# A two-layer hybrid decoder step: decay weights loaded earlier, divisions in a step of their own, other estimates, state work in three insertions

## The chip, the core and the metric

The kernel runs on one core of one Trainium2 chip. Its time is the device time of one launch, in microseconds; before the change the median of three runs is 1157.89 (1155.1 to 1159.74). Five engines with a queue each take part: TensorE (PE in the profile) multiplies, VectorE (DVE), ScalarE (ACT) and GpSimd (POOL) do the elementwise work, and SyncE (SP) issues most transfers. Each engine takes its instructions in the order of its own queue and waits at the first one whose inputs aren't there.

## What is computed

One step of a decoder of two layers, for a prompt of 256 tokens and for 8 samples of 4 tokens with their caches. Both groups go through the same weights as 288 columns of one activation matrix of 1024 rows. Each layer does:

```python
h  = rms(x)
x += W_out( sum_m sigmoid(g_m(h)) * P_m(mixer_m(h)) ),  m in {SWA-GQA+sinks, RG-LRU, GLA}
x += CrossAttn(rms(x), memory K/V)            (4 heads over 256 memory tokens)
x += ConvFFN(rms(x))                          (up-proj -> causal dwconv(3) -> SwiGLU -> down)
```

The change lies in the three mixers. The first is attention in a window of 128 tokens, 8 query heads over 2 key heads, with a sink in the softmax; each sample attends to its cached 128 rows. The second (RG-LRU) is a gated linear recurrence of width 512: two block-diagonal products, sigmoids, an exponential, a square root, and a scan. The third (GLA) is linear attention with a decay, in chunks of 32 tokens:

```python
log_alpha = jax.nn.log_sigmoid((a_c @ p['gla_wa2'] + p['gla_ba']).astype(F32)) / GLA_TAU
q_t = qi * jnp.exp(cum)
k_t = ki * jnp.exp(-cum)
o = jnp.einsum('bhts,bhsv->bhtv', att, vi) + jnp.einsum('bhtd,bhdv->bhtv', q_t, S)
S_new = jnp.exp(last[:, :, 0, :])[..., None] * S + jnp.einsum('bhsd,bhsv->bhdv', ki * jnp.exp(last - cum), vi)
```

For a sample the chunk is its 4 tokens, and `S` is the state that comes in from memory: 8 samples times 4 heads of 64 x 128.

## The kernel before

**The main stream.** The large products run as split fp32: `weights` loads a tile of 512 KB into `wst` (4 buffers), ScalarE rounds it into `whi` (L138), VectorE puts the rest into `wlo` (L139), and `mm3` does three matmuls of 128 x 288 for each block of 128 x 128 (L204 to L206). Such a matmul is called a main matmul below, and places in the program are given by their number: 24 of them use one weight tile. SP issues the tile loads in order, with the smaller loads between them.

**The chains.** Each mixer is a Python generator (`swa`, `lru`, `gla`). A `yield` ends a step, and a step is issued as one piece between two main matmuls. `tick()`, called every few main matmuls, looks at an estimate of the time, `est["pe"]`, and issues the next step of each chain whose `ready` has passed. `account()` keeps the estimate: it adds a duration for each instruction, from its engine and size. So numbers in `account` decide where a step lies among the main matmuls. TensorE's order is fixed by hand in this way; the queues of the other engines are put in order by a scheduler, by priority, and loads may be moved up by `tc.high_priority`.

**What the text below follows.** In layer 0 the chains begin at about main matmul 150, and the mixers end by 1250; layer 1 repeats it at some 3650 more. `gla` begins with L771, which multiplies the low-rank decay input `ac` by `wa2` (its load is L766), then L772 to L777 (log-sigmoid). `swa` takes norms (`head_norm`, whose results go through copies L504 and L505 to the matmul L246), scores (L565), exponentials (L581), divisions by the softmax's sum (L590), transposes (L594) and the product with the values (L604). For the samples: scores L630, softmax L637 to L653, transposes L657 and L658, copies L662 (ScalarE) and L663 (VectorE), products L666 and L670, transposes L677. `lru` has its products at L720 with sigmoids at L721, then L725 and L726 (exponential and tanh), L731 and L734. L1422 is the sigmoid of a branch gate. A change of function on ScalarE can need a table load (ACT_TABLE_LOAD), which the profile lists under the line that follows it. In `gla`, the sample states are loaded, used and updated at L931 to L947, two samples in each of four steps.

The small products write PSUM tiles of a pool of four (`psm`), which come free when the engine that reads them is done.

Of the kernel before, what the change touches and what calls it, by code (L numbers as in the profile page):

```python
# [13 lines left out]
ALU = mybir.AluOpType  # L14
# [7 lines left out]
NB = 8  # L22
# [40 lines left out]
def trunk(ctx: ExitStack, tc: tile.TileContext, a: dict):  # L63
# [32 lines left out]

    def m1(n=T, dt=F32):

        return tp.tile([P, T], dt, tag="m1", bufs=9, name=nm("m1"))[:, :n]

    def g2(w):
        return gp.tile([P, 2, WF], F32, tag="g", name=nm("g")).rearrange("p k t -> p (k t)")[:, :w]
# [43 lines left out]
    def account(i):  # L146

        if not hasattr(i, "engine") or not i.outs or i.opcode == "DMACopy":
            return
        e, n = str(i.engine), 1  # L150
        for _, c in i.outs[0].ap[1:]:
            n *= c
        if i.opcode == "Matmult":
            rows, cols = i.ins[0].ap[0][1], 1
            for _, c in i.ins[1].ap[1:]:
                cols *= c
            if i.ins[0].dtype == F32R:
                c = n / 2400 + 0.012
            elif getattr(i, "is_transpose", False):
                c = 0.109  # L160
            else:
                c = n / 600 * min(1.0, -(-rows // 32) / 4) * min(1.0, -(-cols // 32) / 4)
            est["pe"] = max(est["pe"], est["cur"] or 0.0) + c
            if est["cur"] is not None:
                est["cur"] = est["pe"]
            return
        c = {"EngineType.DVE": 0.1 + n / 850, "EngineType.Activation": 0.22 + n / 1200}.get(e, 0.15 + n / 600)
        cur = est["cur"] if est["cur"] is not None and est["serial"] else est["pe"]
        t = est["busy"][e] = max(est["busy"].get(e, 0.0), cur) + c
        if est["cur"] is not None:  # L170
            est["cur"] = max(est["cur"], t + 0.1)

    nc.push_inst_callback(account)
# [7 lines left out]
    class Chain:  # L181


        def __init__(self, gen):
            self.gen, self.out, self.done, self.ready = gen, None, False, est["pe"]

        def step(self):
            est["cur"] = est["pe"]
# [102 lines left out]
    def head_norm(src, n, scale, nt=T, bw=TB):  # L291

        sq = s5()[:, : n * nt].rearrange("p (j t) -> p j t", t=nt)
        A.activation(sq, src, AF.Square)
        yield
        pss = psm()
        for j in range(n):
            PE.matmul(pss[32 * j : 32 * j + 32, :nt], cc("one32"), sq[:, j], start=True, stop=True, skip_group_check=True)
        yield
        ss = m1(nt)  # L300
        A.copy(ss[: 32 * n], pss[: 32 * n, :nt])
        nb = nt // bw
# [167 lines left out]
    def swa(l, got, Q, KV):  # L470
# [78 lines left out]
        for blk in range(2):  # L549
# [37 lines left out]
            for kv in range(2):  # L587
                for j in range(4):
                    h = kv * 4 + j
                    V.tensor_scalar(pp[kv][:, j, :nk], pp[kv][:, j, :nk], den[:, h : h + 1], None, ALU.mult)  # L590
                for kb in range(blk + 1):
                    ptr = psm()
                    for j in range(4):
                        PE.transpose(ptr[:, j * P : (j + 1) * P], pp[kv][:, j, kb * P : (kb + 1) * P], ident)  # L594
                    if kb == 0:
                        A.copy(ptt[kv][:, kb, :], ptr)
                    else:
                        V.tensor_copy(ptt[kv][:, kb, :], ptr)
                    yield
# [161 lines left out]

    def gla(l, got):

        wa2 = m1(2 * P)
        with tc.high_priority(2 * AHEAD):
            nc.sync.dma_start(wa2, a["wa2"][l])  # L766
        ac = got["ac"]
        zc, za = s5t(), s5t()
        for t in range(2):
            pz = psm()  # L770
            PE.matmul(pz[:, :T], wa2[:, t * P : (t + 1) * P], ac, start=True, stop=True)  # L771
            A.activation(zc[:, t], pz[:, :T], AF.Identity, bias=prm[:, l, C_GBA + t : C_GBA + t + 1])  # L772
        yield

        A.activation(za[:, :2], zc[:, :2], AF.Abs)
# [63 lines left out]
        A.copy(kls, ptr[:, P : 2 * P])  # L839
        yield  # L840

        o = s5()
        os, o = o[:, 8 * P : 9 * P], o[:, : 8 * P].rearrange("p (b i h d) -> p b i h d", b=2, i=2, h=2)
        ss = sm([P, 9], "gss", 1)
# [77 lines left out]
                      skip_group_check=True)  # L922
        V.copy_predicated(atts3, cc("gs").bitcast(I32).rearrange("p (h t) -> p h t", h=4), bc(pa[:, :32], 4))
        yield
        po = psm()
        PE.matmul(po[:, :P], atts, vs, start=True, stop=False, skip_group_check=True)
        for b0 in (0, 4):
            pk = [psm(), psm()]
            for b in (b0, b0 + 2):
                s0 = g2(512).rearrange("p (b h d) -> p b h d", b=2, h=2)  # L930
                nc.sync.dma_start(s0, a["glas"][l, :, b : b + 2])  # L931
                for i in range(2):
                    for h in range(4):
                        PE.matmul(po[32 * h : 32 * h + 32, :P], qg[:, h, 32 * (b + i) : 32 * (b + i) + 32], s0[:, i, h // 2],
                                  start=False, stop=(b + i == NB - 1), skip_group_check=True)
                klm = m1(2 * P).rearrange("p (i d) -> p i d", i=2)
                for i in range(2):
                    V.tensor_scalar(klm[:, i], kls, cc("kb")[:, b + i : b + i + 1], None, ALU.mult)
                for i in range(2):
                    j = b + i - b0  # L940
                    for hp in range(2):
                        rows = slice(hp * 64, hp * 64 + 64)
                        PE.matmul(pk[hp][:, j * P : (j + 1) * P], klm[rows, i], vs[rows], start=True, stop=True)
                for i in range(2):
                    j = b + i - b0
                    for hp in range(2):
                        V.scalar_tensor_tensor(s0[:, i, hp], s0[:, i, hp], elast[:, hp, 8 + b + i : 9 + b + i],  # L947
                                               pk[hp][:, j * P : (j + 1) * P], ALU.mult, ALU.add)
                G.dma_start(a["o_gs"][l, :, b : b + 2], s0)
                yield  # L950
        A.copy(os, po[:, :P])
        A.activation(sqj, po[:, :P], AF.Square, accum_out=ss[:, 8:9])
        yield

        got["gla"] = True

# [374 lines left out]
    def mixers(l):  # L1331
# [37 lines left out]

        pm = psm()  # L1370
        wac = m1(2 * P).rearrange("p (k m) -> p k m", k=KD)
        with tc.high_priority(2 * AHEAD):
            nc.sync.dma_start(wac, a["wac"][l])
        V.tensor_mul(wac, wac, prm[:, l, C_GM : C_GM + KD].unsqueeze(2).to_broadcast([P, KD, 32]))
        for k in range(KD):
            q = 32 * (k % 4)
# [278 lines left out]
```

## Time and profile before

| | |
|---|---|
| median of three runs | 1157.89 us |
| the profiled execution | 1156.28 us |
| its span in the trace | 1154.5 us |
| TensorE busy | 1115.5 us, 97% |
| VectorE, ScalarE, GpSimd busy | 69%, 55%, 22% |
| mean granted TensorE clock | 0.991 of full |

The span is the time from the first to the last instruction in the trace; 1.8 us of the execution lie around it. TensorE runs 97% of the span, so another engine's busy time matters only where TensorE waits for it. A row of a timeline or of the waits gives the time that an engine sat idle ahead of an instruction and what the trace takes for the releaser. A granted clock of 0.50 is TensorE's lower level.

### The profile page before, as it was taken

The page shows a single profiled execution, that of the slowest core. Times are in us where ns is not written, and L with a number is a line of the kernel's source. Part 1 is how long each engine was busy: PE and PEld are TensorE (multiplying, and loading weights), DVE is VectorE, ACT ScalarE, POOL GpSimd, SP SyncE. Part 2 cuts the span into 40 slices and gives each one's busy share as a digit, 9 for nine tenths or more (in the row PEclk, how much of TensorE's full clock was granted, in tenths as well). Part 3 has the DMA queues.
Part 4 walks back from the last instruction along what each step waited for, and adds up shares of the span by engine and source line. Part 5 has one row for each costly group of instructions (what it writes and reads, how often), then busy time and mean ns, then how long its engine had stood idle before and what let it go on. Part 6 is the DMA issues. An engine that isn't in the chain of part 4 may idle for free. (4 is left out here: it accounts for less than half of the span.)

```text
span 1154.5 us, 22367 instructions
## 1 busy us (share of the span) xinstructions
PE 1115.5 (97%) x8846; PEld 1060.2 (92%) x8846; DVE 797.6 (69%) x1454; ACT 630.0 (55%) x971; POOL 258.4 (22%) x426
## 2 busy tenths in 40 slices
PE   9699999999999999999998999999999999999998
PEld 8598789999989999999988987899999899999998
DVE  6666685866665878785466666778576668888743
ACT  6435769444554556564445465674455456656532
POOL 1220100311011355550021201012100014555400
PEclk9899999999999999999999998999999999999999
DMA  8563455567467544556554533645675544555562
GB/s 286 197 192 112 134 165 161 186 193 246 156 217 232 157 147 156 164 150 202 174 167 133 154 97 129 182 166 183 201 246 173 184 141 133 160 164 165 176 197 84
DMA packets 62663, 198.11 MB, mean 172 GB/s; under 512 B 7960, under 2 KB 11768, under 8 KB 62560
## 3 DMA queue, kind: packets, MB, share of 16 engines
q1 hardware_dynamic: 59536, 188.55, 51.5%
q0 software_dynamic: 2880, 8.15, 2.0%
q8 instruction: 69, 1.13, 0.4%
q14 instruction: 34, 0.28, 0.1%
q10 hardware_dynamic: 144, 0.00, 0.0%
HBM read 187.35 MB, written 8.95 MB: 170 GB/s over the span
## 5 line engine op out<-in xcount | busy, mean ns | idle before, releaser
L139 DVE TENSOR_TENSOR wlo<-wst,whi 128x1024 fp32r<-128x1024 f32 (+1 forms) x302 | 370.6, 1229 | 153.1 <-ACT whi L138 152.0
L138 ACT CAST whi<-wst 128x1024 fp32r<-128x1024 f32 (+1 forms) x302 | 312.0, 1035 | 268.2 <-PE mm L205 207.1
L204 PE MATMUL mm<-xh,whi 128*128 128x288 f32 x1488 | 449.2, 302 | 1.5 <-DVE g L1440 1.5
L206 PE MATMUL mm<-xh,wlo 128*128 128x288 f32 x1488 | 443.6, 298 | 0.3 <-DVE wlo L139 0.2
L205 PE MATMUL mm<-xl,whi 128*128 128x288 f32 x1488 | 441.4, 297 | 1.0 <-DVE xl L255 1.0
L204 PEld LDWEIGHTS mm<-xh,whi 128*128 128x128 f32 x1488 | 281.9, 189 | 14.2 <-issue 11.3
L206 PEld LDWEIGHTS mm<-xh,wlo 128*128 128x128 f32 x1488 | 281.5, 189 | 5.0 <-DVE wlo L139 1.3
L205 PEld LDWEIGHTS mm<-xl,whi 128*128 128x128 f32 x1488 | 281.7, 189 | 2.8 <-DVE xl L255 1.9
L204 PE MATMUL mm<-s,whi 128*128 128x288 f32 (+1 forms) x756 | 223.7, 296 | 2.3 <-DVE g L1440 2.3
L205 PE MATMUL mm<-s,whi 128*128 128x288 f32 (+1 forms) x756 | 223.1, 295 | 2.5 <-DVE s L219 2.5
L206 PE MATMUL mm<-s,wlo 128*128 128x288 f32 (+1 forms) x756 | 222.5, 294 | 0.0
L204 PEld LDWEIGHTS mm<-s,whi 128*128 128x128 f32 x756 | 142.3, 188 | 4.5 <-issue 2.3
L205 PEld LDWEIGHTS mm<-s,whi 128*128 128x128 f32 x756 | 142.3, 188 | 4.1 <-DVE s L219 4.0
L206 PEld LDWEIGHTS mm<-s,wlo 128*128 128x128 f32 x756 | 142.2, 188 | 0.5
L1310 DVE SCALAR_TENSOR_TENSOR y<-u,prm,y 128x304 f32<-128x304 f32 x176 | 84.0, 530 | 0.3
L1314 POOL TENSOR_TENSOR m<-y 128x256 f32<-128x256 f32 x44 | 60.6, 1378 | 68.0 <-ACT y L1311 49.8
L218 ACT CAST s<-m 128x288 fp32r<-128x288 f32 (+1 forms) x46 | 19.6, 427 | 78.9 <-POOL m L1315 78.9
L1308 ACT ACTIVATE y<-u,prm 128x304 f32<-128x304 f32 x88 | 51.9, 635 | 11.8 <-DVE u L1301 11.8
L219 DVE TENSOR_TENSOR s<-m,s 128x288 fp32r<-128x288 f32 (+1 forms) x46 | 20.8, 451 | 49.1 <-ACT s L218 49.1
L260 POOL TENSOR_TENSOR s<-s 128x288 f32<-128x288 f32 x20 | 17.6, 879 | 140.0 <-ACT s L259 132.9
L1442 POOL TENSOR_TENSOR g<-g,g 128x576 f32<-128x576 f32 x12 | 25.1, 2092 | 84.4 <-DVE g L1440 60.4
L1294 POOL COPY u<-s 128x32 f32<-128x32 f32 x44 | 41.3, 940 | 0.0
(392 smaller groups left out, 1292.8 us busy)
## 6 DMA issues: line engine op xcount, KB each, us to landing
wst<-in_win SPq DMA_DIRECT2D x98, 512.0 KB, 3.6
wst<-in_up SPq DMA_DIRECT2D x88, 512.0 KB, 3.5
wst<-in_down SPq DMA_DIRECT2D x32, 512.0 KB, 3.6
wst<-in_wbr SPq DMA_DIRECT2D x24, 512.0 KB, 3.5
s<-in_mk SPq DMA_DIRECT2D x16, 512.0 KB, 6.7
wst<-in_wout SPq DMA_DIRECT2D x16, 512.0 KB, 4.1
wst<-in_down SPq DMA_DIRECT2D x16, 384.0 KB, 3.1
g<-in_mv SPq DMA_DIRECT2D x16, 256.0 KB, 3.9
```

What stands on the lines that cost most here:

```text
L138: A.copy(hi[:, :n], st[:, :n])
L139: (E or V).tensor_sub(lo[:, :n], st[:, :n], hi[:, :n].bitcast(F32))
L204: PE.matmul(out, wh, bh, start=first, stop=False)
L205: PE.matmul(out, wh, bl, start=False, stop=False)
L206: PE.matmul(out, wl, bh, start=False, stop=last)
L218: A.copy(hi, src)
L219: V.tensor_sub(lo, src, hi.bitcast(F32))
L1294: G.tensor_copy(us[:, :, :, 0:2], fhist[:, 2 * c : 2 * c + 2])
L1308: A.activation(y[:, i, :WFO], u[:, i, 2:], AF.Identity, scale=w[2], bias=prm[:, l, C_FCB + f : C_FCB + f + 1])
L1310: V.scalar_tensor_tensor(y[:, i, :WFO], u[:, i, j : j + WFO], w[j], y[:, i, :WFO], ALU.mult, ALU.add)
L1314: G.tensor_mul(h[:, :NP_], y[:, 0, :NP_], y[:, 1, :NP_])
L1442: (G if x == 1 or m < KD - 4 else V).tensor_add(acc[m], acc[m], g)
```

## The change

- `wa2` is loaded in `mixers` next to `wac`, with a higher priority. In `gla` both products of L771 come first, then both activations.
- `head_norm` has one more `yield`, behind the copy of the sums.
- In `swa` all divisions of L590 are one step, and the transposes come in the steps after it.
- In `gla` the four loads of the sample states come before the prompt's loop. The products `klm` have a step of their own; then one step has all 32 products with the states, and the first updates; a second has the remaining updates.
- `account` no longer moves TensorE's estimate up to the chain's own time, takes other durations for VectorE and ScalarE, and leaves GpSimd out of a chain's time. A chain's first step waits for VectorE's estimate plus 0.5.
- The pool `m1` has ten buffers in place of nine.

```diff
-            est["pe"] = max(est["pe"], est["cur"] or 0.0) + c
+            est["pe"] += c
             if est["cur"] is not None:
-                est["cur"] = est["pe"]
+                est["cur"] = max(est["cur"], est["pe"])
             return
-        c = {"EngineType.DVE": 0.1 + n / 850, "EngineType.Activation": 0.22 + n / 1200}.get(e, 0.15 + n / 600)
+        c = {"EngineType.DVE": 0.09 + n / 970, "EngineType.Activation": 0.12 + n / 1200}.get(e, 0.15 + n / 600)
...
-        if est["cur"] is not None:
+        if est["cur"] is not None and not (est["serial"] and e == "EngineType.Pool"):
             est["cur"] = max(est["cur"], t + 0.1)
...
-            self.gen, self.out, self.done, self.ready = gen, None, False, est["pe"]
+            self.gen, self.out, self.done = gen, None, False
+            self.ready = max(est["pe"], est["busy"].get("EngineType.DVE", 0.0)) + 0.5
...
                     V.tensor_scalar(pp[kv][:, j, :nk], pp[kv][:, j, :nk], den[:, h : h + 1], None, ALU.mult)
+                yield
+            for kv in range(2):
                 for kb in range(blk + 1):
...
-        wa2 = m1(2 * P)
-        with tc.high_priority(2 * AHEAD):
-            nc.sync.dma_start(wa2, a["wa2"][l])
-        ac = got["ac"]
+        ac, wa2 = got["ac"], got["wa2"]
...
+        s0 = []
+        for b in range(0, NB, 2):
+            s0.append(g2(512).rearrange("p (b h d) -> p b h d", b=2, h=2))
+            nc.sync.dma_start(s0[-1], a["glas"][l, :, b : b + 2])
...
+        klm = []
+        for b in range(0, NB, 2):
+            klm.append(m1(2 * P).rearrange("p (i d) -> p i d", i=2))
+            for i in range(2):
+                V.tensor_scalar(klm[-1][:, i], kls, cc("kb")[:, b + i : b + i + 1], None, ALU.mult)
+        yield
         po = psm()
         PE.matmul(po[:, :P], atts, vs, start=True, stop=False, skip_group_check=True)
+        for b in range(NB):
+            for h in range(4):
+                PE.matmul(po[32 * h : 32 * h + 32, :P], qg[:, h, 32 * b : 32 * b + 32], s0[b // 2][:, b % 2, h // 2],
+                          start=False, stop=(b == NB - 1), skip_group_check=True)
...
         for b0 in (0, 4):
             pk = [psm(), psm()]
-            for b in (b0, b0 + 2):
-                s0 = g2(512).rearrange("p (b h d) -> p b h d", b=2, h=2)
-                nc.sync.dma_start(s0, a["glas"][l, :, b : b + 2])
...
         wac = m1(2 * P).rearrange("p (k m) -> p k m", k=KD)
-        with tc.high_priority(2 * AHEAD):
+        got["wa2"] = m1(2 * P)
+        with tc.high_priority(3 * AHEAD):
             nc.sync.dma_start(wac, a["wac"][l])
+            nc.sync.dma_start(got["wa2"], a["wa2"][l])
```

Three places show what this does to the queues. SP's queue in layer 0, before, from the load of the convolution history on (`wax` is for the recurrence, `swav` and `mk` are caches for the sample attention and the cross attention, `wst` is a weight tile):

```order
L1393 DMA lhist_774<-in_lconv 128x96
L697 DMA s_1717<-in_wax 128x1024
L137 DMA wst_706<-in_win 128x1024
L699 DMA lh_1719<-in_lh 128x32
L617 DMA s_1813<-in_swav 128x1024
L1103 DMA s_3008<-in_mk 128x1024
L766 DMA m_457<-in_wa 128x256
L1103 DMA s_3010<-in_mk 128x1024
```

The same queue after the change, at the load of `wac`:

```order
L137 DMA wst_449<-in_win 128x1024
L1379 DMA m_402<-in_wac 128x256
L1380 DMA m_403<-in_wa 128x256
L137 DMA wst_531<-in_win 128x1024
L137 DMA wst_595<-in_win 128x1024
L467 DMA prm<-in_prm 128x250
```

The load of `wa2` stands thirteen places earlier, ahead of all the others of the first piece.

VectorE's queue in layer 1, at the second block of `swa`, before (`g` with `elast` are updates of the sample states, `s` divided by `den` the softmax, `wlo` the low part of a weight tile):

```order
L947 SCALAR_TENSOR_TENSOR g_8065<-g_8065,elast_7237,sm_8063 128x128
L947 SCALAR_TENSOR_TENSOR g_8065<-g_8065,elast_7237,sm_8064 128x128
L1421 TENSOR_TENSOR g_8129<-mm_7995,rbc_6901 128x2x288
L139 TENSOR_TENSOR wlo_8304<-wst_8302,whi_8303 128x1024
L590 TENSOR_SCALAR s_7782<-s_7782,den_7780 128x256 x2
L590 TENSOR_SCALAR s_7783<-s_7783,den_7780 128x256 x4
```

The same place after (the divisions are L592 there):

```order
L139 TENSOR_TENSOR wlo_8181<-wst_8179,whi_8180 128x1024
L586 TENSOR_TENSOR den_7792<-den_7792,es_7793 128x8
L587 RECIPROCAL den_7792<-den_7792 128x8
L592 TENSOR_SCALAR s_7794<-s_7794,den_7792 128x256 x4
L592 TENSOR_SCALAR s_7795<-s_7795,den_7792 128x256 x4
L954 SCALAR_TENSOR_TENSOR g_7560<-g_7560,elast_7269,sm_8081 128x128
```

The divisions no longer stand behind a gate's product and a weight tile; the state updates come behind them.

ScalarE's queue in layer 1, at the sample attention, before, up to L721 of the recurrence (`es`, `mx`, `den` are the softmax of the samples):

```order
L642 ACT_TABLE_LOAD
L642 ACTIVATE es_8421<-mx_8419,prm 128x2
L644 ACTIVATE m_8418,den_8420<-m_8418,mx_8419 128x132 x2
L138 CAST whi_8617<-wst_8616 128x1024
L1422 ACT_TABLE_LOAD
L1422 ACTIVATE g_8480<-g_8480 128x2x288
L218 CAST s_8333<-s_8332 128x1152
L138 CAST whi_8663<-wst_8662 128x1024
L662 COPY m_8558<-sm_8539 128x256
L721 ACTIVATE s_8544<-sm_8546,prm 128x312
```

After, from the second of the two exponentials of that softmax (L648 there) to the copy that was L662 (L666 there; L725, L729 and L730 are what was L721, L725 and L726):

```order
L648 ACTIVATE m_8530,den_8532<-m_8530,mx_8531 128x132
L725 ACT_TABLE_LOAD
L725 ACTIVATE s_8486<-sm_8564,prm 128x312
L725 ACTIVATE s_8487<-sm_8567,prm 128x312
L729 ACT_TABLE_LOAD
L729 ACTIVATE s_8588<-s_8486,sp_85 128x312 x2
L730 ACTIVATE s_8486<-s_8486,sp_85 128x312 x2
L729 ACTIVATE s_8588<-s_8486,sp_85 128x312
L1429 ACT_TABLE_LOAD
L1429 ACTIVATE g_8598<-g_8598 128x2x288
L730 ACTIVATE s_8486<-s_8486,sp_85 128x312
L666 COPY m_8620<-sm_8583 128x256
```

The copy stood two table loads behind the exponentials' first, ahead of the recurrence; now much of the recurrence, with three table loads, stands between. On TensorE, L630 and L657 have 18 main matmuls between them, where they had 66.

## Rows read from the trace of the kernel before

**Rows 1.** The page's first part: busy us, share of the span, instructions.

```profile
PE 1115.5 (97%) x8846; PEld 1060.2 (92%) x8846; DVE 797.6 (69%) x1454; ACT 630.0 (55%) x971; POOL 258.4 (22%) x426
```

**Rows 2.** TensorE's waits: line and releaser, us in all, times, longest.

```profile
PE sm L771 <- DVE m L509: 9.5, 1, 9.5
PE sm L594 <- DVE s L590: 6.4, 4, 2.3
PE sm L771 <- DVE s L509: 4.1, 1, 4.1
...
PE sm L666 <- DVE m L663: 0.8, 2, 0.4
...
PE sm L926 <- DVE m L923: 0.8, 2, 0.4
...
PE sm L969 <- DVE s L958: 0.7, 2, 0.4
```

**Rows 3.** Timeline of SP's queue, 30 to 35 us: start, duration, instruction.

```profile
33.24 0.33 SPq L766 DMA_DIRECT2D m<-in_wa  x1
```

**Rows 4.** The line L766, first in layer 0, then in layer 1.

```profile
DMA to landing us min/median/max: 7.1/7.1/7.1
...
DMA to landing us min/median/max: 3.5/3.5/3.5
```

**Rows 5.** Timeline of TensorE at L771 in layer 0; idle time before, releaser.

```profile
40.48 1.78 PE L771 MATMUL sm<-m,m 128*128 128x288 f32 x3 [9.54 <-DVE m L509]
```

**Rows 6.** Windows: us, TensorE busy (instructions), granted clock, DMA share, GB/s.

```profile
40.48:44.10 3.62, 3.62 (x11) 0.50 0.58 201
137.00:144.00 7.00, 6.98 (x89) 1.00 0.37 114
609.97:614.10 4.13, 4.13 (x16) 0.59 0.01 2
706.30:713.10 6.80, 6.77 (x42) 0.50 0.40 118
```

**Rows 7.** Timeline of VectorE ahead of L594 in layer 0.

```profile
135.48 1.23 DVE L139 TENSOR_TENSOR wlo<-wst,whi 128x1024 fp32r<-128x1024 f32 x1
```

**Rows 8.** Timeline of ScalarE around L771 in layer 0.

```profile
33.71 0.21 ACT L336 ACTIVATE sl<-prm 128x8 f32<-128x8 f32 x1 [2.21 <-DMA prm<-in_prm]
...
44.03 0.69 ACT L776 ACTIVATE s<-s 128x576 f32<-128x576 f32 x1
```

**Rows 9.** Timeline of ScalarE at the sample attention in layer 1.

```profile
736.24 1.28 ACT L642 ACT_TABLE_LOAD   x1
737.54 0.30 ACT L642 ACTIVATE es<-mx,prm 128x2 f32<-128x2 f32 x1
...
742.50 1.04 ACT L138 CAST whi<-wst 128x1024 fp32r<-128x1024 f32 x1
743.45 0.36 ACT L662 COPY m<-sm 128x256 f32<-128x256 f32 x1
743.81 1.05 ACT L721 ACTIVATE s<-sm,prm 128x312 f32<-128x312 f32 x2
```

**Rows 10.** Timeline of VectorE at the sample attention in layer 1.

```profile
740.90 0.15 DVE L646 TENSOR_TENSOR den<-den,es 128x2 f32<-128x2 f32 x1
...
741.69 0.31 DVE L653 TENSOR_TENSOR pn<-m,cst 128x32 f32<-128x32 f32 x2
```

**Rows 11.** Timeline of TensorE in layer 1: main matmuls, L630, L720.

```profile
702.98 0.29 PE L205 MATMUL mm<-xl,whi 128*128 128x288 f32 x1
...
703.51 0.30 PE L206 MATMUL mm<-xh,wlo 128*128 128x288 f32 x1
...
732.79 0.66 PE L630 MATMUL sm<-s,m 128*32 128x132 f32 x16
...
743.08 1.22 PE L720 MATMUL sm<-s,s 128*128 128x312 f32 x4
```

**Rows 12.** Timeline of ScalarE in layer 0, the recurrence's first L721 and last L726.

```profile
171.63 1.05 ACT L721 ACTIVATE s<-sm,prm 128x312 f32<-128x312 f32 x2
...
186.03 0.99 ACT L726 ACTIVATE s<-s,sp 128x312 f32<-128x312 f32 x2
```

More of the change, by code (lines that the diff above doesn't have):

```diff
@@ L97, in m1 @@
     def m1(n=T, dt=F32):
-        return tp.tile([P, T], dt, tag="m1", bufs=9, name=nm("m1"))[:, :n]
+        return tp.tile([P, T], dt, tag="m1", bufs=10, name=nm("m1"))[:, :n]
     def g2(w):
@@ L762, in gla @@
     def gla(l, got):
-        wa2 = m1(2 * P)
-        with tc.high_priority(2 * AHEAD):
-            nc.sync.dma_start(wa2, a["wa2"][l])
-        ac = got["ac"]
+        ac, wa2 = got["ac"], got["wa2"]
         zc, za = s5t(), s5t()
+        pz = [psm(), psm()]
         for t in range(2):
-            pz = psm()
-            PE.matmul(pz[:, :T], wa2[:, t * P : (t + 1) * P], ac, start=True, stop=True)
-            A.activation(zc[:, t], pz[:, :T], AF.Identity, bias=prm[:, l, C_GBA + t : C_GBA + t + 1])
+            PE.matmul(pz[t][:, :T], wa2[:, t * P : (t + 1) * P], ac, start=True, stop=True)
+        for t in range(2):
+            A.activation(zc[:, t], pz[t][:, :T], AF.Identity, bias=prm[:, l, C_GBA + t : C_GBA + t + 1])
         yield
@@ L924, in gla @@
         yield
+        klm = []
[3 more added lines that the diff above has]
+                V.tensor_scalar(klm[-1][:, i], kls, cc("kb")[:, b + i : b + i + 1], None, ALU.mult)
+        yield
         po = psm()
         PE.matmul(po[:, :P], atts, vs, start=True, stop=False, skip_group_check=True)
+        for b in range(NB):
+            for h in range(4):
+                PE.matmul(po[32 * h : 32 * h + 32, :P], qg[:, h, 32 * b : 32 * b + 32], s0[b // 2][:, b % 2, h // 2],
+                          start=False, stop=(b == NB - 1), skip_group_check=True)
@@ L927, in gla @@
+        A.copy(os, po[:, :P])
+        A.activation(sqj, po[:, :P], AF.Square, accum_out=ss[:, 8:9])
         for b0 in (0, 4):
             pk = [psm(), psm()]
-            for b in (b0, b0 + 2):
-                s0 = g2(512).rearrange("p (b h d) -> p b h d", b=2, h=2)
-                nc.sync.dma_start(s0, a["glas"][l, :, b : b + 2])
[L932 to L950, printed above, removed]
@@ L951, in gla @@
-        A.copy(os, po[:, :P])
-        A.activation(sqj, po[:, :P], AF.Square, accum_out=ss[:, 8:9])
-        yield
+            for j in range(4):
+                for hp in range(2):
+                    rows = slice(hp * 64, hp * 64 + 64)
+                    PE.matmul(pk[hp][:, j * P : (j + 1) * P], klm[(b0 + j) // 2][rows, j % 2], vs[rows], start=True, stop=True)
+            for j in range(4):
+                b = b0 + j
+                for hp in range(2):
+                    V.scalar_tensor_tensor(s0[b // 2][:, b % 2, hp], s0[b // 2][:, b % 2, hp], elast[:, hp, 8 + b : 9 + b],
+                                           pk[hp][:, j * P : (j + 1) * P], ALU.mult, ALU.add)
+                if j % 2:
+                    G.dma_start(a["o_gs"][l, :, b - 1 : b + 1], s0[b // 2])
@@ L955, in gla @@
+            yield
         got["gla"] = True
```

## The prediction

> **What bounds the kernel now.** I read the page's busy table first, then TensorE's waits, then the timelines of the two places that wait longest. TensorE is busy for 1115.5 of 1154.5 us [rows 1], so time can come only from its idle 39 us and from stretches at the lower clock. The table of waits says where it is idle: L771 waits 9.5 and 4.1 us, L594 6.4 us in four waits, L666, L926 and L969 0.8, 0.8 and 0.7 us [rows 2]. The releaser that it names for L771, a VectorE product at L509, is the wrong one. The matmul reads the decay weights `wa2`, whose load SP issues at 33.24 us [rows 3] and which lands 7.1 us later [rows 4], at 40.3; the matmul starts at 40.48 [rows 5]. In layer 1 the same load takes 3.5 us, and L771 starts as it lands. In SP's queue the load stands behind a 512 KB load for the cross attention, which nobody wants yet.
>
> The second loss is the clock. In three stretches the granted clock was at or near half, 1.2 GHz for 2.4: 0.50 for 3.62 us behind the 9.5 us wait, 0.59 for 4.13 us behind the 4.1 us wait, 0.50 for 6.80 us behind L594's 2.3 us wait in layer 1 [rows 6]. The twin of that last wait in layer 0, at 137 us, cost no clock (1.00).
>
> **Part 1, `wa2` loaded in `mixers`.** The load now stands right behind `wac`, thirteen places earlier in SP's queue, and L771 sits 24 main matmuls later in layer 0 and 12 in layer 1. The waits of 9.54 and 4.13 us go: −13.7. The load's 128 KB stay the same. Next late in layer 0 is L246 at main matmul 204, which reads ScalarE's copies of L504 and L505. Before, these ran in the shadow of the wait. Now ScalarE does, behind L771, the second L772, L775, L776 and L777 (0.5 to 0.69 each), a table load (1.28), a weight cast (1.04), L504 and L505 (0.36 each) [rows 8, 9], about 5.7 us, while TensorE has 30 main matmuls (4.0) and a few small ones. I take 1.4 us of wait. Bounds: 0, if the copies come ahead of the table load's end; 4, if L336, which stands ahead of all this in ScalarE's queue and was held until 33.71 by `prm` [rows 8], is held some 2.6 us longer.
>
> **Part 2, divisions in a step of their own.** In the second block of `swa`, L590's division for one half of the heads stood in VectorE's queue behind L139 (1.23 us from 135.48) [rows 7], and L594 waited for it. Now all divisions are issued a step earlier, and the transposes stand several main matmuls behind. The 6.4 us go. No instruction is added.
>
> **Part 3, the estimate and the three insertions.** As many instructions run; they stand elsewhere. L926 moves from main matmul 666 to 630 but its input L921 by 84, and L969 from 744 to 762, so each has about a microsecond more than the 0.4 it lacked: −1.5. The four state loads go out between weight tiles that are loaded three tiles ahead, where the DMA share is 0.37 [rows 6]. I cost them at nothing, since that lead covers them; without it 1 MB a layer at 201 GB/s [rows 6] would cost up to 5 us. The tenth `m1` buffer, the yield in `head_norm` and the early products `klm` move work, and add none.
>
> What the moves cost lies at the end of the mixers. Before, L630 (scores of the sample attention) and L657 (its transposes) were 66 main matmuls apart, and the pairs of L720 (products of the recurrence) came behind L657. Now they are 18 apart in both layers, with L720 between and ahead of them, and all that the two chains need of ScalarE meets in one queue. I add up from the first L720 of the stretch: 1.28 a table load, 0.5 each for L721, L725, L726 and for L644 with its read, 0.3 L642, 1.04 a cast, 0.36 L662 [rows 9], 0.69 L1422 (as large as L776) [rows 8], 1.2 a pair of L720, 0.7 L630 and, from the two main matmuls four places apart, 0.1325 each of these [rows 11], 1.1 on VectorE from L646 to the end of L653 [rows 10], and an estimated 0.4 for its copy L663, by ScalarE's L662.
>
> Layer 1: TensorE comes to L657 at 9.5 us. ScalarE has two L721, a cast, a table load, L725 and L726 done by 5.2, a table load and four L721 by 8.4, a table load, L642 and the first L644 by 10.5, a cast by 11.5, the second L644 by 12.0. VectorE, with the cast's low part first, ends L653 at 13.9: a wait of 4.4. Then come a table load and two L721 (14.2), a table load and five of L725 and L726 (18.0), a table load, L1422, L726 and L662 (20.8), and L663 (21.2). TensorE comes to L666 at 15.9: a wait of 5.3. Layer 0 by the same sum: 1.2 at the second half of an L720, whose PSUM tile is free only behind two table loads; 1.5 at L657; 5.2 at L666. Together 9.7 and 7.9: +17.6. The old 0.8 at L666 goes: −0.8. From below this is bounded by the 0.8 that the two chains cost when apart. From above by 28: the same ScalarE work lay from 171.63 to 187.02 in layer 0 [rows 12], and with that whole length on the path each layer loses about 14.
>
> A rule of the skill speaks against this part. In the rows a table load lasts 1.28 us and the next activation starts 0.02 us behind its end (736.24, 737.54) [rows 9]. The Trainium skill, "ScalarE: Activation LUTs", section "What ACT_TABLE_LOAD costs", adds a drain to every switch and comes to 2.66 us. By the rows the eleven table loads of the two stretches are 14.1 us of ScalarE, by the page 29.3, and the sum would be 15 us later. The rows show no room for the drain and decide.
>
> **Clock.** With the three old waits go 3.62/2 = 1.8, 4.13 × 0.41 = 1.7 and 6.80/2 = 3.4 [rows 6]: −6.9. For the new waits I give back 1.7 behind each L666 and half of that behind L246: +4.2. Bounds: 0, and 10.2 (3.4 at each of the three).
>
> **Sum**, from the profiled execution's 1156.3 (1.6 below the median shown, 1157.89): −13.7 − 6.4 − 1.5 − 0.8 − 6.9 = −29.3, and 1.4 + 17.6 + 4.2 = +23.2. So 1150.2 for a profiled execution, and 1151.8 on the median's scale.
>
> **Rivals.** *A: the new waits don't come.* All of −29.3 stays but L246's 1.4 and a little clock: 1130. For it: before, the same two chains cost 0.4 us a layer [rows 2]. Against it: the queue, in which L662 and the second L644 now stand behind eleven table loads in all. 17%.
>
> *B: ScalarE's queue ahead of L662 is longer than my sum (slower).* The place is the stretch from L720 to L666 in both layers; each microsecond by which ScalarE is later there goes to TensorE at full price, since the program puts nothing else in its way. It decides from 5.9 us more a layer, about 1.1 us more for each table load. At 1.4 us more for each the sum is 15 us later: 1167. For it: I add mean durations, and the weight casts stand in the same path. Against it: the gap of 0.02 us behind a table load. The page on activation tables, named above, gives this price. 14%.
>
> *C: the clock stays low.* Behind L246 and both L666 the clock stays at half for as long as behind the worst wait of before, 10.2 us lost in place of 4.2: 1158, no change. For it: a wait of 2.3 us was enough at 706 us. Against it: the same wait at 137 us cost nothing. The Trainium skill, "TensorE: Matmul & The Clock Gate", section "A second HAM failure mode: psum-queue depth-cycling", says that frequent short idles between groups of matmuls make the clock swing; two or three waits in one stretch would be such a pattern, and no place in the trace of before shows one. 14%.
>
> **How the numbers follow.** The forecast has 55%, with 1144 to 1160 as its own range (the bounds of L246, 2 us either way for each layer's pile-up, the clock). Half a per cent, 5.8 us, is about what a measurement of this kernel can tell from no change, so below 1152.1 is faster and above 1163.7 slower. The forecast lies on the edge: 30 of its 55 are faster, 25 the same. A is faster (17), C the same (11) or slower (3), B slower (14). That makes 0.47, 0.36 and 0.17. The range of 8 in 10 reaches some way towards A and to B's near end: 1136 to 1165.
>
> **What would show it.** Right: no wait of L771 over 0.5 us, none of L594, no half clock at 40 and 610 us, and in their place waits of 1 to 6 us at L657 and L666 (lines 661 and 670 of the changed file), released by VectorE behind ScalarE's work, in both layers. Wrong: L666 within 1 us of its turn (then A), a wait at L771 still there, or an activation that starts over a microsecond behind its table load (then B). If the span falls by over 20 us, ScalarE's order around L662 was not what bound that stretch.

## The result, and the profile after

The changed kernel takes 1140.59 us (median of 4 runs, 1138.72 to 1141.97), the kernel before in the same job 1157.07 (1155.10 to 1159.74). The ratio is 0.9855, with a 95% interval of 0.983 to 0.988: faster by 16.5 us. The forecast, 6.1 us faster, had the direction, and the time lies in its range; the size was off by ten us. The profiled execution's span fell from 1154.5 to 1137.6, by 16.9.

The first part of the page after, which answers to [rows 1]:

```profile
PE 1107.2 (97%) x8846; PEld 1060.8 (93%) x8846; DVE 795.9 (70%) x1454; ACT 624.8 (55%) x967; POOL 255.9 (22%) x426
```

TensorE is busy 8.3 us less with the same number of instructions, so half of the gain is not in the idle time that the list of waits shows. TensorE's waits after (line and releaser, us in all, times, longest), which answer to [rows 2]:

```profile
PE sm L670 <- DVE m L667: 9.1, 2, 5.4
PE sm L634 <- DMA s<-in_swak: 5.2, 2, 2.9
PE sm L661 <- DVE m L653: 3.3, 2, 3.0
...
PE sm L247 <- ACT m L506: 0.6, 1, 0.6
PE mm L205 <- DVE g L1428: 0.5, 1, 0.5
...
PE sm L1027 <- DVE rm L1023: 0.2, 1, 0.2
```

What was L771 (L772 now) and L594 (L598) is gone from the list. In their place stand the three lines of the sample attention: its scores L634, its transposes L661, its first products L670, 17.6 us in all. Two waits that the forecast left alone also shrank, of a gate at L204 and of a norm at L1022; they are L205 with 0.5 and L1027 with 0.2 now. Before, the same view had:

```profile
PE mm L204 <- DVE g L1440: 3.8, 4, 1.5
...
PE sm L1022 <- DVE rm L1018: 1.6, 1, 1.6
```

The load of `wa2`, now L1380, and the four stretches at half clock (columns: us; busy time and instructions of TensorE, of its weight loads, of VectorE, ScalarE and GpSimd; granted clock; DMA share; GB/s):

```profile
L1380 SPq DMA_DIRECT2D m<-in_wa x2: 422/423/424, 17.5 to 576.0; - x2
```

```profile
172.88:179.70 6.82, 6.06 (x36) 5.42 (x37) 2.49 (x3) 5.59 (x8) 0.16 (x1) 0.50 0.24 77
719.01:722.42 3.41, 3.41 (x12) 2.68 (x11) 0.52 (x5) 1.04 (x2) 0.24 (x1) 0.50 0.66 211
729.25:732.66 3.41, 3.41 (x15) 3.04 (x14) 1.46 (x1) 3.38 (x7) 0.00 (x0) 0.50 0.42 150
736.08:742.90 6.82, 6.51 (x38) 5.87 (x39) 3.40 (x4) 4.79 (x5) 0.40 (x2) 0.50 0.23 79
```

The load goes out at 17.5 us where it went out at 33.24 [rows 3]. The clock is at 1.2 GHz for 20.5 us behind the waits at L670 (both layers), L634 and L661 (layer 1).

To see where the time went, I compare the two traces by the number of the main matmul (there are 7296 in both, in the same order) and take the time from one number to another:

| stretch, main matmuls | before, us | after, us | change | forecast |
|---|---|---|---|---|
| 0 to 1200: opening, mixers of layer 0 | 222.20 | 212.73 | -9.5 | -3.8 |
| 1200 to 3200: cross attention, feed-forward | 295.35 | 291.37 | -4.0 | 0 |
| 3200 to 4800: opening, mixers of layer 1 | 270.13 | 269.39 | -0.7 | -2.2 |
| 4800 to 7296: cross attention, feed-forward | 358.16 | 355.49 | -2.7 | 0 |

The forecast's column is its own sum, put into these stretches. It misses 5.6 us in the mixers of layer 0 and 6.7 in two stretches where it expected nothing, and was 1.5 too hopeful in the mixers of layer 1.

### The profile page after: what moved, and what is told of

Same layout as the page of the kernel before. It is cut to its first block, busy times and chain, and to the rows that moved or that the text cites. A ratio compares the mean times of both kernels' runs of the same rounds, so it can differ in the third digit from the quotient of the medians.

```text
span 1137.6 us, 22359 instructions
## 1 busy us (share of the span) xinstructions
PE 1107.2 (97%) x8846; PEld 1060.8 (93%) x8846; DVE 795.9 (70%) x1454; ACT 624.8 (55%) x967; POOL 255.9 (22%) x426
## 5 line engine op out<-in xcount | busy, mean ns | idle before, releaser
L205 PE MATMUL mm<-xh,whi 128*128 128x288 f32 x1488 | 450.1, 302 | 0.0
L207 PE MATMUL mm<-xh,wlo 128*128 128x288 f32 x1488 | 441.2, 297 | 0.0
L205 PEld LDWEIGHTS mm<-xh,whi 128*128 128x128 f32 x1488 | 282.3, 190 | 12.2 <-issue 9.9
L207 PEld LDWEIGHTS mm<-xh,wlo 128*128 128x128 f32 x1488 | 282.1, 190 | 0.3
L205 PE MATMUL mm<-s,whi 128*128 128x288 f32 (+1 forms) x756 | 223.6, 296 | 0.5 <-DVE g L1428 0.5
L207 PE MATMUL mm<-s,wlo 128*128 128x288 f32 (+1 forms) x756 | 222.3, 294 | 0.0
L205 PEld LDWEIGHTS mm<-s,whi 128*128 128x128 f32 x756 | 142.2, 188 | 2.6 <-issue 2.0
L207 PEld LDWEIGHTS mm<-s,wlo 128*128 128x128 f32 x756 | 142.1, 188 | 0.5
L261 POOL TENSOR_TENSOR s<-s 128x288 f32<-128x288 f32 x20 | 17.5, 876 | 140.8 <-ACT s L260 140.8
L1299 POOL COPY u<-s 128x32 f32<-128x32 f32 x44 | 44.4, 1010 | 0.6 <-DMA s<-in_fconv 0.6
L1449 POOL TENSOR_TENSOR g<-g,g 128x576 f32<-128x576 f32 x12 | 21.9, 1828 | 90.4 <-DVE g L1447 90.4
```

The source lines that it names most:

```text
L205: PE.matmul(out, wh, bh, start=first, stop=False)
L207: PE.matmul(out, wl, bh, start=False, stop=last)
L1299: G.tensor_copy(us[:, :, :, 0:2], fhist[:, 2 * c : 2 * c + 2])
L1449: (G if x == 1 or m < KD - 4 else V).tensor_add(acc[m], acc[m], g)
```

## Experiments

### Each part alone, on the kernel before

**The loads alone (`e1_wa2`).**

```diff
-        wa2 = m1(2 * P)
-        with tc.high_priority(2 * AHEAD):
-            nc.sync.dma_start(wa2, a["wa2"][l])
-        ac = got["ac"]
+        ac, wa2 = got["ac"], got["wa2"]
...
+            nc.sync.dma_start(got["wa2"], a["wa2"][l])
```

> The kernel before with the decay weights loaded in mixers beside wac, both products of L771 first, and ten m1 buffers; estimate, divisions and state work as before. My theory: L771's two waits (13.7 us) and the half clock behind them (3.5 us) go, and a wait of 1 to 3 us at L246 in layer 0 comes, so 1141 to 1144 us. Rival, that L771 waits for VectorE as the table of waits says: both waits stay above 3 us and the time falls by under 5 us. On the feed-forward part, where the changed kernel takes 6.35 us for a pair of weight tiles and the kernel before 6.52: if the tenth m1 buffer does that, it shows here (5 to 6 us more); if the estimate does it, the pairs stay at 6.52 us.

Measured 1150.34 us (1145.38 to 1152.26), ratio 0.9922 [0.9895, 0.9949]. The forecast was 1141 to 1144, a miss of size. L771's waits of 13.6 us are gone, and so, without the divisions' step, are the 6.4 us of L594; only some 8 us arrive. The waits of this run show why:

```profile
PE sm L932 <- DMA g<-in_glas: 6.4, 2, 4.1
PE sm L658 <- DVE pn L653: 4.7, 2, 2.4
```

With TensorE earlier, the sample states (L932) and the sample attention (L658) are late, which had no wait before. The half clock did not go either: four stretches at other places make 20.5 us at 0.50, with TensorE busy for 19.1 of them, where it was busy for 13.8 us at 0.50 before. A wait that goes uncovers the next.

**The divisions alone (`e2_div`).** The diff is the one `yield` behind the divisions in `swa`, with a loop of its own for the transposes.

> The kernel before with the divisions in a step of their own, nothing else. My theory: the four waits of L594 (6.4 us) go, and with them the half clock behind 706 us (3.4 us): 1147 to 1149 us. Rival, that VectorE has no room there and the transposes wait for the divisions wherever they stand: L594 still waits 3 us or more and the time falls by under 4 us.

Measured 1166.91 us (1164.71 to 1168.03), ratio 1.007 [1.0045, 1.0095]: slower, a miss of sign. L594 (L596 here) does not wait any more, and yet:

```profile
PE mm L204 <- ACT s L218: 12.9, 2, 6.5
PE sm L773 <- DMA m<-in_wa: 9.4, 1, 9.4
```

The list puts L773's wait, L771 before, down to the load of `wa2`, as the prediction had read it. The new wait comes from the later steps, which all move back: the scores of the samples from main matmul 780 to 852, VectorE's last product of the recurrence from 1045 to 1104. That product is so late that the branch product behind it waits. Timelines of layer 0, VectorE, ScalarE and TensorE:

```profile
210.37 2.20 DVE L747 TENSOR_TENSOR_SCAN s<-s,s 128x312 f32<-128x312 f32 x3
...
214.29 1.21 DVE L754 TENSOR_TENSOR s<-s,s 128x1024 f32<-128x1024 f32 x1
...
216.29 1.15 ACT L218 CAST s<-s 128x1152 fp32r<-128x1152 f32 x1 [4.34 <-POOL s L756]
...
217.50 0.61 PE L204 MATMUL mm<-s,whi 128*128 128x288 f32 x1 [6.50 <-ACT s L218]
```

The scan ends at 212.6, its product at 215.5; a short GpSimd product (L756) follows, the cast begins at 216.29, and TensorE loses 6.50 us. Layer 1 has the same wait. What was won at L594 was paid twice at the end of the mixers. What the step costs is therefore not a term of its own: it depends on the main matmul at which the account then issues each later step.

**The account alone (`e3b_new_est`),** with the chain's readiness rule: the first three pieces of the diff ahead of the prediction.

> The kernel before with the changed account and Chain.ready alone. My theory now: the estimate alone makes the feed-forward pairs 6.35 in place of 6.52 us (5 to 6 us in all) and takes away the 1.5 us waits of the branch products and at L1022 (4 to 5 us); it also brings L630 and L657 nearer (48 main matmuls) with a part of the pile-up on ScalarE (5 to 12 us of waits and clock). L771 waits as before. So 1148 to 1160 us. Rival, that the feed-forward part's gain comes from the tenth m1 buffer or from the mixers' earlier end: its pairs stay at 6.52 us here.

Measured 1153.97 us (1147.26 to 1155.01), ratio 0.9947 [0.9928, 0.9967], in the expected range, though L771 (L772 here) waits 7.0 us and not as before. The weight loads' rows (PEld) show what the forecast did not see, here of the page before, which the prediction did not read:

```profile
L206 PEld LDWEIGHTS mm<-xh,wlo 128*128 128x128 f32 x1488 | 281.5, 189 | 5.0 <-DVE wlo L139 1.3
```

and of this run (L207 is the same product):

```profile
L207 PEld LDWEIGHTS mm<-xh,wlo 128*128 128x128 f32 x1488 | 280.7, 189 | 0.4
```

Before, one product of each pair of tiles found its low part just not ready: in VectorE's queue the low part stood behind the products that form the convolution's input. A row of VectorE before, in the feed-forward of layer 0, and TensorE's matmul that reads it:

```profile
438.80 1.22 DVE L139 TENSOR_TENSOR wlo<-wst,whi 128x1024 fp32r<-128x1024 f32 x1
...
440.07 0.40 PE L206 MATMUL mm<-xh,wlo 128*128 128x288 f32 x1
```

The low part ends at 440.02 and the matmul starts at 440.07, behind one at 439.87; the next starts 0.24 later, not 0.13. Most pairs of tiles (48 main matmuls) took 6.52 us where the 0.1325 of [rows 11] make 6.36; after the change most take 6.35. The tenth `m1` buffer has no part in it: `e1_wa2` has that buffer, and its pairs take 6.52.

VectorE did not become faster. The order of its queue here is the same after the change, and one turn of it takes 6.51 us. Two turns before, then after:

```profile
437.63 0.46 DVE L219 TENSOR_TENSOR s<-m,s 128x288 fp32r<-128x288 f32 x1 [1.21 <-ACT s L218]
...
444.14 0.46 DVE L219 TENSOR_TENSOR s<-m,s 128x288 fp32r<-128x288 f32 x1 [1.21 <-ACT s L218]
```

```profile
424.18 0.46 DVE L220 TENSOR_TENSOR s<-m,s 128x288 fp32r<-128x288 f32 x1 [1.21 <-ACT s L219]
...
430.69 0.46 DVE L220 TENSOR_TENSOR s<-m,s 128x288 fp32r<-128x288 f32 x1 [1.21 <-ACT s L219]
```

What the account gives is a head start. VectorE's first product of the feed-forward comes at main matmul 2176 in the kernel before, in `e1_wa2`, in `e2_div` and in `e3_old_est` below, all with the old account; with the new one, after the change and in this run, it comes at 2152 (layer 1: 5824 and 5800). TensorE then gains some 0.17 us on VectorE with each pair until it has caught up. Of the 21 pairs from 2208 on, they take over 6.4 us from the fourth on before, and from the eighteenth on after. By these numbers the loss would come back in a longer feed-forward.

**All but the account (`e3_old_est`):** the changed kernel with the old account and rule.

> The changed kernel with the old account of engine times and the old readiness rule of the steps, so loads, divisions and three insertions alone. Theory (the new account is worth the feed-forward's 5.7 us and the waits at L1428/L1440 and L1022 or L1027, together about 10 us): 1148 to 1153 us, feed-forward pairs of tiles at 6.52 us again with a wait for the low part in each pair. Rival (the account is worth only what it is worth alone, in the kernel before: a ratio of 0.995, 6 us): 1144 to 1148 us.

Measured 1150.63 us (1148.88 to 1150.88), ratio 0.9937 [0.9921, 0.9954]: the theory's range, so the account is worth 10.0 us in the changed kernel and, alone, 4.5 (by the medians) to 6.1 (by the ratio). The old loss in the feed-forward is back. The sample attention waits less than after the change, but the branch product behind it now waits 6.7 us, and 30.7 us are at half clock where the change has 20.5:

```profile
PE sm L660 <- DVE m L652: 9.1, 2, 4.5
PE mm L204 <- ACT s L218: 6.7, 2, 3.4
...
PE sm L1026 <- DVE rm L1022: 1.6, 1, 1.6
```

Between main matmuls 2300 and 3200 this run takes 122.44 us, as the kernel before; the changed one 119.59.

### What the pile-up at the sample attention is made of

**The old insertions (`e4_old_states`):** the changed kernel with the state work of before, in four steps, each with its load.

```diff
-        s0 = []
-        for b in range(0, NB, 2):
-            s0.append(g2(512).rearrange("p (b h d) -> p b h d", b=2, h=2))
-            nc.sync.dma_start(s0[-1], a["glas"][l, :, b : b + 2])
...
+            for b in (b0, b0 + 2):
+                s0 = g2(512).rearrange("p (b h d) -> p b h d", b=2, h=2)
+                nc.sync.dma_start(s0, a["glas"][l, :, b : b + 2])
```

> The changed kernel with the old state work: loads in the steps, four insertions with 8 products and 4 products each. My theory: the insertions themselves cost: about 5 to 6 us of TensorE time come back (two thirds of it in the stretches of the state work, the rest where chains move), so 1144 to 1147 us, with waits as in the changed kernel within 3 us. Rival, that the saving came from where the insertions stand and not from their number: within 2 us of the changed kernel.

Measured 1132.89 us (1130.78 to 1136.39), ratio 0.9792 [0.9754, 0.983]: 7 to 8 us faster than the change (by the ratios or the medians), a miss of sign. The three insertions do save time where they stand: their products L941 and L950 are busy 3.9 and 4.6 us after, 5.1 and 5.7 with four steps, and the quarter of the mixers around them (main matmuls 4128 to 4368) takes 49.03 us against 50.84. But with three steps the sample attention's own steps stand closer together: its scores L634 and transposes L661 are 18 main matmuls apart in both layers after the change, 42 and 36 in this run. Between 4464 and 4584 the change takes 38.90 us, this run 27.29. The load of the cached keys also has more time, 6.9 us from its issue to the scores' turn in layer 0 where the change leaves 3.4. The edit moves the state loads and the products `klm` as well, and no run separates these from the number of steps. Its list has no wait at the scores, and one each at the two others:

```profile
PE sm L670 <- DVE m L667: 4.0, 1, 4.0
PE sm L661 <- DVE m L653: 3.0, 1, 3.0
...
PE mm L205 <- DVE g L1444: 2.4, 3, 1.5
```

**One activation table (`e8_one_table`).** The changed kernel with exp and tanh of the recurrence and exp of the sample softmax replaced by sigmoid, and the square root by a square, so this kernel leaves the reference's functions out; TensorE's order is the same.

```diff
-            A.activation(av[:, t], r[:, t], AF.Exp, scale=sp8[:, l, t : t + 1])
-            A.activation(r[:, t], r[:, t], AF.Tanh, scale=sp8[:, l, t : t + 1])
+            A.activation(av[:, t], r[:, t], AF.Sigmoid, scale=sp8[:, l, t : t + 1])
+            A.activation(r[:, t], r[:, t], AF.Sigmoid, scale=sp8[:, l, t : t + 1])
```

> The changed kernel with the exponentials and the tanh of the recurrence and of the sample softmax replaced by sigmoids, and the square root by a square, so that no table load stands among them; TensorE's order is the same, the values are not. My theory, that ScalarE's queue holds L661 and L670 and its table loads are a third of it: five loads (6.4 us) go from the stretch in layer 0 and six (7.7 us) in layer 1, so the waits of L661 and L670 fall from 12.4 us to under 3, the half clock behind them mostly goes, and the time is 1117 to 1128 us. Rival, that the late load of the cached keys (named for L634's 5.2 us) sets the end of the stretch: L661 and L670 still wait over 6 us together and the time stays above 1134 us.

Measured 1124.02 us (1122.58 to 1125.62), ratio 0.9696 [0.9677, 0.9716], as the theory of ScalarE's queue has it. The waits at L661 fell off the list, and those at L670 came down from 9.1 to 2.3; the keys' load stays late at L634:

```profile
PE sm L634 <- DMA s<-in_swak: 2.8, 1, 2.8
...
PE sm L670 <- DVE m L667: 2.3, 2, 1.5
```

ScalarE's timeline in layer 0, after the change, around the copy L666 that L670 waits for:

```profile
166.56 1.28 ACT L725 ACT_TABLE_LOAD   x1
167.86 0.94 ACT L725 ACTIVATE s<-sm,prm 128x312 f32<-128x312 f32 x2
168.68 0.56 ACT L730 ACTIVATE s<-s,sp 128x312 f32<-128x312 f32 x1
169.25 1.28 ACT L729 ACT_TABLE_LOAD   x1
170.55 1.00 ACT L729 ACTIVATE s<-s,sp 128x312 f32<-128x312 f32 x2
171.45 0.99 ACT L730 ACTIVATE s<-s,sp 128x312 f32<-128x312 f32 x2
172.34 0.54 ACT L729 ACTIVATE s<-s,sp 128x312 f32<-128x312 f32 x1
172.79 0.35 ACT L666 COPY m<-sm 128x256 f32<-128x256 f32 x1
```

ScalarE does not stop once from 166.56 to 172.79, with two table loads of 1.28 us and the recurrence ahead of the copy. In `e8_one_table`, which has no table load in this stretch, the copy starts at 169.31.

**The copy ahead of the recurrence (`e6b`).** The changed kernel; exp and tanh of the recurrence are issued only when the sample attention's products are.

```diff
+        while "swas" not in got:
+            yield
         for t in range(4):
```

> The changed kernel with the exponentials and tanh of the recurrence (L729, L730) issued only when the sample attention has issued L670 and L674. My theory: ScalarE's copy for L670 comes up to five activations and a table load earlier in layer 0, so its wait falls from 5.4 to 1 to 3 us there, with less in layer 1; 1130 to 1137 us. Rival, that the recurrence is what ends the mixers: what is won at L670 comes back as a wait of the second branch's first product, and the time stays within 3 us of the changed kernel.

Measured 1132.57 us (1129.95 to 1136.47), ratio 0.9767 [0.9733, 0.9801], as expected: L670's wait falls from 9.1 to 2.2 us, with as many table loads (36) in the whole kernel. In layer 0 all four of the recurrence's exponentials stood ahead of the copy; now three of them stand behind it. The same work in another order of ScalarE's queue takes most of the wait away. A new wait of 2.6 us stands at a branch gate (L1431).

**Both chains apart (`e64`).** The kernel of `e4_old_states` with the recurrence's products, too, behind the sample attention.

> The kernel of e4_old_states with all of the recurrence's products (L724 there, L727 here) issued behind L670 and L674, so that the two chains use ScalarE one after the other. My theory: the waits of 4.0 and 3.0 us at L670 and L661 and the half clock behind them (5 us) go; the recurrence has 24 us left to the second branch in each layer and needs about as much, so a wait of up to 4 us a layer can come there: 1122 to 1131 us. Rival, that apart the two chains are too long for the stretch: the branch waits 5 us or more a layer and the time is 1133 us or above.

Measured 1137.87 us (1134.65 to 1139.68), ratio 0.9813 [0.9789, 0.9836] where it was 0.9792 without the move: no gain, and the rival holds. L670 waits 0.6 us, but the branch product at the end of the mixers now waits for the recurrence:

```profile
PE mm L205 <- ACT s L219: 5.4, 2, 3.3
PE mm L206 <- DVE s L220: 4.6, 8, 1.1
```

**The same hold in the kernel with four steps (`e6b4`),** the lines of `e6b` in that of `e4_old_states`.

> The four-step state work of before in the changed kernel (1132.9 us), and in it the recurrence's activations L729/L730 held until the sample attention's products are issued. Theory (exp and tanh of the recurrence stand in front of the sample attention's copies and reciprocals): the wait at L670, 3.96 us at 164.70, falls below 1.5 and the half clock there goes (3.4 us): 1126 to 1131 us. Rival (in this order the sample attention's own chain is the later one; the recurrence only becomes later): the branch products wait for the scan's result by 2 us or more and it measures 1132 to 1138 us.

Measured 1130.56 us (1129.92 to 1135.77), ratio 0.9782 [0.9753, 0.9811], within the interval of `e4_old_states`. The wait at L670 is still 3.95 us (3.96 without the hold): a miss of the mechanism, though the time lies in the theory's range. ScalarE's timeline shows that the hold moved nothing there:

```profile
158.06 1.28 ACT L732 ACT_TABLE_LOAD   x1
159.36 0.56 ACT L732 ACTIVATE s<-s,sp 128x312 f32<-128x312 f32 x1
159.93 1.28 ACT L726 ACT_TABLE_LOAD   x1
...
163.00 0.37 ACT L666 COPY m<-sm 128x256 f32<-128x256 f32 x1
```

The exponential (L729, here L732) and its two table loads still stand ahead of the copy, as in `e4_old_states`. It is the only one of the four that stood there, and one stays ahead in `e6b` too, so the hold had nothing to move.

**The cached keys from another queue (`e9_swak_pool`).** The changed kernel with one line other:

```diff
-        nc.sync.dma_start(ks[:, :, :P], a["swak"][l])
+        G.dma_start(ks[:, :, :P], a["swak"][l])
```

> The changed kernel with the cached keys of the sample attention loaded through GpSimd's queue, which is idle there, in place of SP's, where they stand behind weight tiles. Rival to my theory: the 5.2 us of L634 go and nothing takes their place, with the half clock behind 719 us: 1133 to 1135 us. My theory: L634's waits go, but L661 and L670 wait longer by most of it, since ScalarE's queue ends at nearly the same time; 1137 to 1141 us.

Measured 1136.1 us (1135.05 to 1139.59), ratio 0.9806 [0.9784, 0.9828]: 4.5 us (medians) to 5.7 (ratios) off the change. The median lies between the two ranges; the waits below decide for the rival, and the theory is a miss. After the change SP has the load behind two weight tiles, and GpSimd's queue in this run sends it earlier. Timeline of SP after the change, then of GpSimd in this run:

```profile
148.50 6.00 SPq L137 DMA_DIRECT2D wst<-in_win  x2
154.55 0.65 SPq L620 DMA_DIRECT2D s<-in_swak  x1
```

```profile
146.90 0.92 POOL L620 DMA_DIRECT2D s<-in_swak  x1 [14.98 <-PE sm L598]
```

The wait at L634 goes (5.2 us) and so does the half clock behind it in layer 1. The waits at L661 and L670 do not take its place; they stay, at 3.9 and 8.9 us where they were 3.3 and 9.1.

**Hold and queue together (`e12_gate_pool`),** the edits of `e6b` and `e9_swak_pool`.

> Theory (the waits of the changed kernel's pile-up are separate and add up): with the recurrence's activations issued behind the sample attention and the cached keys loaded by GpSimd's queue, both savings stand together: the gated kernel measured 1132.6 us and has two waits for the keys left, 5.0 us (1.69 and 3.35), with a stretch at half clock that begins at the second (3.4 us, worth 1.7); expected 1126 to 1130 us, no wait at L634, L670 at most 2.5 us. Rival (what is late next takes it): the row maxima or the transposes at L661 are waited for instead and it stays at 1131 to 1134 us.

Measured 1127.81 us (1126.64 to 1128.38) against 1158.12 for the kernel before in the same job, ratio 0.9742 [0.9726, 0.9757]: the fastest version that leaves nothing out, 2.6% below before and some 1.1% below the change. The two savings add up, as the theory said. Its waits:

```profile
PE sm L661 <- DVE m L653: 3.9, 2, 3.1
PE mm L205 <- DVE g L1431: 2.6, 1, 2.6
...
PE sm L670 <- DVE m L667: 2.0, 1, 2.0
```

## Why the prediction was right, and where its sizes were wrong

**Part 1 and the old waits: right.** L771 (13.6 us) and L594 (6.4 us) lost their waits, and the half clock behind them went. L594's go in `e1_wa2` as well as in `e2_div`, so the runs do not say which part of the change takes them. L246 (L247 now) waits 0.6 us, not 1.4.

**The pile-up: right in mechanism, and in sum by luck.** The forecast had 17.6 us of new waits at the sample attention and the recurrence, all from ScalarE's queue; the trace has 17.6, but only the 12.4 at L661 and L670 come from that queue. In layer 0 the forecast for L666 (L670) was a wait of 5.2; measured, it is 5.38. That ScalarE's queue makes it is shown by `e8_one_table` and `e6b`. The other parts are smaller than forecast: L670 in layer 1 waits 3.7 us, not 5.3, the recurrence's product has no wait (forecast 1.2), and L657 (L661) waits 3.3 in all, not 5.9. The wait of 5.2 us at the scores, for the cached keys, happens to fill the gap.

**That a load is moved away from a matmul costs nothing: right for the states, but the forecast did not look at the keys.** Their load takes 5.0 to 5.6 us to land. Before, it went out 6.2 us ahead of the scores in both layers; after the change it has 3.4 us to the scores' turn in layer 0 and 2.2 in layer 1. In layer 0 it goes out at 154.55 us, before at 154.4, while the turn comes 2.6 us earlier. The load became late because the work that reads it came forward by more than the load did.

**The term that failed most: the account, which the forecast put at nothing.** The forecast used Part 3's account only to see where steps land ("As many instructions run; they stand elsewhere"). By `e3_old_est` it is worth 10.0 us: 6.0 of it in the feed-forward, where VectorE's head start brings most of the weights' low parts in time (main matmuls 2300 to 3200 and 5800 to 6800: 122.44 to 119.59 and 135.77 to 132.61 us), 1.4 at the norm's matmul (L1022, now L1027), the rest in the mixers. The gates' wait at L204, 3.8 us in the list before, went too, but it is gone in `e3_old_est` as well (0.3) and mostly gone with the account alone (1.1 in `e3b_new_est`), so no one part can be named for it. The loss in the feed-forward could be read before: 900 main matmuls at 0.1325 [rows 11] are 119.3 us, and the trace had 122.44. The waits' list showed 0.2 us of it: in [rows 11] a matmul lasts 0.29 to 0.30 us and one starts every 0.1325, so one that starts 0.07 late leaves hardly any idle time.

**The insertions: a gain missed, and a larger loss.** That no instruction is added was right, but products side by side in one step take less: by 1.1 to 1.2 us for each of two kinds of products (`e4_old_states`). Against the four steps the three cost 7 to 8 us in all. That this comes from the distance between the sample attention's steps fits the 18 main matmuls against 42 and 36, but is argued, not shown alone.

**The clock: undersized.** The forecast gave back 4.2 us. The four stretches are 20.5 us at half clock; less the 1.1 in which TensorE was waiting anyway, half of the rest is 9.7. Each stretch behind L670 was 6.8 us long, where I had taken 3.4, and L634 and L661 added two of 3.4. This is why layer 1 fell short. It is nearly the 10.2 us of rival C, at other places: none behind L247, and two stretches behind waits that C did not have.

**The stretches, added up.** Layer 0's missing 5.6 us: about 2.1 in waits of the branch products, 0.8 at L247, and 2.6 at the insertions (main matmuls 480 to 720 take 49.69 us in `e4_old_states`, 47.10 after the change); clock and pile-up took 0.6 more than forecast, and some 0.7 stays unexplained. Feed-forward and cross attention: 6.7, made of the 6.0 above and the 1.4 at the norm, less some 0.7 elsewhere. Layer 1's +1.5: clock +5.0, waits of gates -1.4, insertions -1.8, the pile-up -0.2. So some 16 us of gains that the forecast did not have stand against 5.5 us of clock that it had too small; that they partly cancel is luck, and keeps the time inside the range.

**The rivals.** A (no new waits, 1130) is wrong: they came. Yet two small edits behind the change come to 1128. B (a longer queue by a drain at each table load) is wrong: by the timeline above the activation starts 0.02 us behind the end of a load of 1.28 (166.56 and 167.86), as before the change, and the load at 169.25 starts 0.01 us behind the end of the activation ahead of it; the 2.66 us that the Trainium skill states ("ScalarE: Activation LUTs", "What ACT_TABLE_LOAD costs") are not to be seen here. C was right about the price of the clock (9.7 us, it had 10.2) and wrong about the time, 1158, since gains that no rival had came on top.

What stays open: which of the account's numbers gives VectorE its head start in the feed-forward; the runs changed the account only as a whole.

## What to carry to other kernels

In a kernel whose steps are issued by an account of engine times, a part's price can't be read by itself: the same extra step cost 0.7% alone, and the account that was worth 4.5 to 6 us alone was worth 10 beside the rest. Beside the list of waits, divide the time of a uniform stretch by its matmuls and compare that with the best rate in the trace: that shows losses too short to be waits. When such a loss goes, ask whether its cause is gone or only a head start was won. And where work is brought forward, look at every transfer it reads, and at whose activations stand ahead of its copies in the queue.

## What the runs showed of the hardware

The length of a stretch at half clock does not follow from the wait ahead of it. A wait of 5.38 us at 173.64 and one of 3.68 at 736.39 were each met by 6.8 us at 0.50, as was, before the change, one of only 2.3 at 706 [rows 6]; waits of 2.90 (717.94) and 2.95 (728.90) in layer 1 by 3.4 each; the wait of 2.31 us at 160.27 in layer 0 cost no clock at all, while one of 1.98 at 170.09 in `e12_gate_pool` was followed by this (columns as above):

```profile
172.14:175.56 3.42, 2.95 (x14) 2.67 (x13) 0.51 (x1) 3.07 (x7) 0.08 (x1) 0.50 0.46 153
```
